# A hybrid decoder trunk on one core: element-wise work of the token mixers moves from GpSimd to VectorE and ScalarE

## Chip, core and metric

The kernel runs on one core of a Trainium2 chip. The metric is the device time of one execution in microseconds (us). The engines are TensorE (PE; its weight loads are PEld), VectorE (DVE), ScalarE (ACT), GpSimd (POOL) and SyncE (SP), which here issues the DMAs.

## What is computed

One inference step of a two-layer decoder for a prompt of 512 positions and 8 single-position samples, 520 columns in all. Each layer has a SwiGLU feed-forward block (FFN), a mixer with three branches, and a second FFN. The parts of the mixer that the change touches:

```python
def hgrn2_mixer(xq, xf, xi, xg, s0, lb, norm_g):
    k = (1.0 - lbh) * jax.nn.sigmoid(-zf)
    o, S = gla_chunked(heads(xq), k, heads(xi), logf, s0)   # S = f * S + k v^T
    o = o * lax.rsqrt(jnp.mean(o * o, axis=-1, keepdims=True) + EPS)
    o = o * norm_g.reshape(HG_HEADS, HG_DV)
    o = o.reshape(B, L, HG_WIDTH) * jax.nn.silu(xg)

def gmlp_mixer(xu, xv, ws, bs, ng, nb):
    u = jax.nn.gelu(xu)
    v = layer_norm(jax.nn.gelu(xv), ng, nb)
    return u * (tril(ws) v + bs), v          # in chunks of 128 positions

def s5_mixer(...):                           # complex diagonal recurrence
    _, h = lax.associative_scan(_ssm_combine, (a, bu), axis=1)
    y = real(c h) + d_skip * u
    z = jax.nn.gelu(y)
    zz = z @ glu_w + glu_b
    return zz[..., :S5_WIDTH] * jax.nn.sigmoid(zz[..., S5_WIDTH:])

def decoder_layer(...):
    gates = jax.nn.sigmoid(gate_cols).reshape(B, L, N_BRANCH, D_MODEL)
    merged = jnp.einsum('blnd,blnd->bld', gates, bproj)
    x = x + rms_norm(merged @ w_out, norm_g[3])
```

## The kernel before

Activations lie with channels on the 128 partitions and the 520 columns along the free axis, worked in two halves of 256 and 264 columns. Every large product is made of three matmuls: each weight block is loaded as `raw` (SP), cast to a high part `whi` (ACT, L98) and a low part `wlo` (raw minus whi, L102 on DVE or, with `share=True`, L232 on POOL through the helper `ptt`); each activation is split in the same way by `split` (high part on ACT, L110; low part on POOL, or on the engine that is passed, L111). `mm3` (L117, L118, L120) multiplies high with high, low with high and high with low.

Work that is not such a product runs as generators (`s5_scan`, `hgrn_head`) that are advanced from `tick` between weight blocks. The order on each engine is then set by a scheduler, which places instructions by a model of the engines, so an edit can move instructions that it does not name. Each engine executes its own queue strictly in that order.

A mixer goes through these steps:

- `s5_project` makes the S5 inputs. `s5_scan` (L776 on) works 8 steps per layer. In each, PE projects (L790), ACT copies the result to `w` (L792), DVE and POOL rotate it (L811 to L820), DVE scans it (L824), DVE and POOL rotate it back into `w` (L833 to L837), and PE multiplies `w` with tables (L846 to L848). A gelu follows (`gelu2`: square on ACT, L241; two operations on DVE, L244 and L245; tanh on ACT, L246; one on DVE, L247).
- `hgrn_head` runs once per head, 4 per layer. It has 7 levels; in each, PE makes a product of `q` and `k` (L1088), POOL multiplies `k` by the tree of decays (`ptt`, so the profile names L232), DVE multiplies `q` (L1091) and writes the masked result (L1092). The transpose of `k` (L1106) and the final products follow. Its inner function `state` updates two samples' states at a time: three POOL products on 128x256 tiles (`st` by `fs`, `vb` by `ks`, and their sum). `st` and `vb` arrive by DMA.
- `ev_f` and `ev_g` in `hgrn_operands` make `f`, `k` and `sg` for a head: sigmoids on ACT, scale and offset on DVE (L1003, L1004), `sg` on POOL. `stat` and `rstd` (L220 to L228) make the reciprocal root from column means on PE (L256).
- `s5_glu`, `gate`, `gmlp_values`, `gmlp_norm` and `gmlp_mix` follow, then the output product.

The two lines of the state update and of the gelu that matter most:

```python
self.ptt(st, st, bc(fs), ALU.mult)            # POOL, as are the next two
nc.vector.tensor_scalar(t, t, GELU_A, 1.0, ALU.mult, ALU.add)
nc.vector.tensor_tensor(t, t, x, ALU.mult)
```

Of the kernel before, what the change touches and what calls it, by code (L numbers as in the profile page):

```python
# [18 lines left out]
P = 128  # L19
# [23 lines left out]
class Trunk:  # L43
# [190 lines left out]
    def gelu2(self, out, x, pool, tag, bufs=1, scale=None, src=None):  # L234

        nc = self.nc
        shape = [P] + [int(n) for n in x.shape[1:]]
        n = x.shape[0]
        t = pool.tile(shape, F32, tag=tag, name=tag, bufs=bufs)[:n]
        if src is None:  # L240
            nc.scalar.activation(t, x, AF.Square)  # L241
        else:
            nc.scalar.activation(t, src, AF.Square, scale=scale)
        nc.vector.tensor_scalar(t, t, GELU_A, 1.0, ALU.mult, ALU.add)  # L244
        nc.vector.tensor_tensor(t, t, x, ALU.mult)  # L245
        nc.scalar.activation(t, t, AF.Tanh, scale=GELU_B)  # L246
        nc.vector.scalar_tensor_tensor(out, t, 1.0, x, ALU.add, ALU.mult)  # L247

    def stat(self, acc, half, mean, col=None):


        n = 2 + half
        v = self.pxt()
        mm = self.nc.tensor.matmul
        for i in range(n):
            mm(v[:, i:i + 1], acc[:, 128 * (i % 2):128 * (i % 2) + 128], mean, start=True, stop=True)  # L256
        if half:
# [458 lines left out]
    def mixer_units(self, l):  # L716
        return [lambda i=i, m=m: self.unit(self.t["w_in"][l, m], 8, 128, share=i % 2 == 0) for i, m in enumerate((0, 1, 2, 3, 8))]
# [50 lines left out]
    def s5_scan(self, l, pool):  # L768
# [32 lines left out]
        for s in range(n):  # L801
# [9 lines left out]
            self.ptt(tc_[:, 1], wp[:, 1], si[:, 1], ALU.mult)  # L811
            v.tensor_tensor(ta, wp, co, ALU.mult)
            v.tensor_tensor(tc_[:, 0], wp[:, 0], si[:, 0], ALU.mult)
# [19 lines left out]
            self.ptt(tc_[:, 1], ta[:, 1], si[:, 1], ALU.mult)  # L833
            v.tensor_tensor(tc_[:, 0], ta[:, 0], si[:, 0], ALU.mult)
# [46 lines left out]
    def s5_glu(self, l):  # L881
        nc, t = self.nc, self.t
        self.c = []
        for m in range(4):
# [9 lines left out]
            for half in (0, 1):  # L894
                s, b = self.tmph("sil", half), self.tmph("vb", half)
                p1, p2 = ps[half]
                nc.scalar.activation(s, p2, AF.Sigmoid, bias=self.glub[:, l * 8 + 4 + m:l * 8 + 5 + m])
                nc.vector.scalar_tensor_tensor(b, p1, self.glub[:, l * 8 + m:l * 8 + m + 1], s, ALU.add, ALU.mult)
                self.split(c[:, :, SL[half]], b)
# [73 lines left out]
    def hgrn_values(self, l, hh, pool, V):  # L973
# [12 lines left out]
        self.tok_proj("w_i", l, hh, evac, hh == 0)  # L986
# [4 lines left out]
    def hgrn_operands(self, l, h, pool):  # L991
# [5 lines left out]
        def ev_f(half, p):  # L997
# [5 lines left out]
            v.tensor_scalar(fs, fs, lb1, lb, ALU.mult, ALU.add)  # L1003
            v.tensor_scalar(ks, ks, lb1, None, ALU.mult)  # L1004
# [4 lines left out]
        def ev_g(half, p):  # L1009
# [3 lines left out]
            self.ptt(sg[:, SL[half]], a, b, ALU.mult)  # L1013
# [3 lines left out]
    def hgrn_head(self, l, h, V, q, k, f, sg, pool, last):  # L1017
# [60 lines left out]
        for lev in range(7):  # L1078
# [11 lines left out]
            self.ptt(kv, kv, Tr, ALU.mult)  # L1090
# [47 lines left out]
        for half in (0, 1):  # L1138
            st = self.stat(sqs[half], half, self.mean_h)
# [4 lines left out]
            self.split(ap[:, :, SL[half]], b)  # L1144
# [3 lines left out]
    def gmlp_values(self, l, pool):  # L1148
# [3 lines left out]
        for cg in range(2):  # L1152
            def evac(i, p):
# [4 lines left out]
                self.gelu2(self.vt[i][:n, 256 * cg:256 * cg + 256], x, pool, "gt", 2, rc, p)  # L1158
# [29 lines left out]
    def gmlp_mix(self, l, pool, fill):  # L1188
# [11 lines left out]
        for gr in range(4):  # L1200
# [24 lines left out]
            self.split(b[:, :, :NT], mx)  # L1225
# [3 lines left out]
    def mixer(self, l, xd, finish, ahead):  # L1229
# [8 lines left out]
        def head(h, done=0):  # L1238
# [7 lines left out]
            for block, ev in list(zip((8, 4, 12), evs))[done:]:  # L1246
                self.proj_block(l, block + h, ev, h == 0)
# [202 lines left out]
```

## Time and profile before

| | |
|---|---|
| median of 3 runs | 2754.24 us (2752.72 to 2756.12) |
| the profiled execution's own time | 2757.39 us |
| its span, first to last instruction | 2755.3 us |
| PE busy | 2673.8 us, 97% of the span |
| DVE / ACT / POOL busy | 1557.5 / 1014.9 / 795.2 us |

Busy is the time in which an engine had an instruction in work. Matmuls overlap in the pipeline, so the count of matmuls per microsecond says more of PE's pace than its busy time. In the trace each fp32 matmul of the small products appears twice. The profile's span and the runs' times differ by a few microseconds; differences are taken within the same kind.

### The profile page before, as it was taken

Reading aid. Unit: us, or ns where it says so; the run is one execution under the profiler, and the core shown is the slowest. Engines: PE = TensorE matmul, PEld = TensorE weight load, DVE = VectorE, ACT = ScalarE, POOL = GpSimd, SP = SyncE. Lnnn points to the kernel's source line nnn. Section 1 sums busy time; section 2 is a strip of 40 time slices with the busy share of each in tenths; the row PEclk is TensorE's granted clock in tenths of the full one; section 3 lists DMA queues with packets and bytes.
Section 4 is the critical chain, followed back from the end, with each engine's and each line's share of the span. In section 5 each row is a group of like instructions: output and inputs, shape, how many; then the busy total and the mean of one; then the engine's idle time right before and its main releaser. Section 6 shows DMA issues by size and latency. Waiting matters only on the chain. (4 is left out here: it accounts for less than half of the span.)

```text
span 2755.3 us, 54254 instructions
## 1 busy us (share of the span) xinstructions
PE 2673.8 (97%) x21976; PEld 2649.0 (96%) x21976; DVE 1557.5 (57%) x3127; ACT 1014.9 (37%) x2014; POOL 795.2 (29%) x1033
## 2 busy tenths in 40 slices
PE   7999999899999999999999999998999999999998
PEld 7999999889999999999999999998999999999998
DVE  7677867865574564344473434668555654634444
ACT  4344444333243353322343323433323334433232
POOL 5478812453221112011121101145521311301010
PEclk9999999999999999999999999999999999999999
DMA  4344543542232323232322222445332223222321
GB/s 135 102 141 148 160 135 121 182 126 83 86 93 92 116 77 93 93 92 100 93 77 93 90 95 93 131 135 156 98 100 86 87 92 120 84 89 88 99 91 54
DMA packets 131706, 291.16 MB, mean 106 GB/s; under 512 B 19024, under 2 KB 59760, under 8 KB 131456
## 3 DMA queue, kind: packets, MB, share of 16 engines
q1 hardware_dynamic: 131456, 287.70, 33.1%
q8 instruction: 173, 2.83, 0.4%
q14 instruction: 77, 0.63, 0.1%
HBM read 256.97 MB, written 30.67 MB: 104 GB/s over the span
## 5 line engine op out<-in xcount | busy, mean ns | idle before, releaser
L117 PE MATMUL mm<-h,whi 128*128 128x256 f32 (+1 forms) x4224 | 1057.9, 287 | 18.2 <-ACT h L298 7.0
L118 PE MATMUL mm<-h,wlo 128*128 128x256 f32 (+1 forms) x4224 | 1047.1, 284 | 1.1 <-DVE wlo L102 1.1
L117 PEld LDWEIGHTS mm<-h,whi 128*128 128x128 f32 x4224 | 801.6, 190 | 20.2 <-ACT h L298 7.0
L118 PEld LDWEIGHTS mm<-h,wlo 128*128 128x128 f32 x4224 | 804.0, 190 | 1.7 <-DVE wlo L102 1.6
L98 ACT CAST whi<-raw 128x1024 fp32r<-128x1024 f32 (+1 forms) x424 | 437.3, 1032 | 510.9 <-PE mm L120 432.7
L102 DVE TENSOR_TENSOR wlo<-raw,whi 128x1024 fp32r<-128x1024 f32 (+1 forms) x385 | 474.0, 1231 | 233.1 <-ACT whi L98 230.3
L120 PE MATMUL mm<-h,whi 128*128 128x256 f32 (+1 forms) x4224 | 594.5, 283 | 0.0
L120 PEld LDWEIGHTS mm<-h,whi 128*128 128x128 f32 x4224 | 543.1, 189 | 0.0
L111 POOL TENSOR_TENSOR hid<-vb,hid 128x256 fp32r<-128x256 f32 (+1 forms) x132 | 132.7, 1006 | 870.0 <-ACT hid L110 857.0
L117 PE MATMUL mm<-hid,whi 128*128 128x256 f32 (+1 forms) x1408 | 349.0, 284 | 3.6 <-ACT hid L110 3.6
L118 PE MATMUL mm<-hid,wlo 128*128 128x256 f32 (+1 forms) x1408 | 347.5, 283 | 0.0
L124 DVE TENSOR_TENSOR va<-mm,r 128x256 f32<-128x256 f32 (+1 forms) x320 | 136.1, 426 | 310.3 <-PE mm L120 304.0
L117 PEld LDWEIGHTS mm<-hid,whi 128*128 128x128 f32 x1408 | 265.6, 189 | 3.8 <-ACT hid L110 3.8
L118 PEld LDWEIGHTS mm<-hid,wlo 128*128 128x128 f32 x1408 | 266.2, 189 | 0.0
L120 PE MATMUL mm<-hid,whi 128*128 128x256 f32 (+1 forms) x1408 | 201.2, 283 | 0.3 <-DVE hid L111 0.3
L124 DVE TENSOR_TENSOR vb<-mm,r 128x256 f32<-128x256 f32 (+1 forms) x176 | 74.9, 425 | 192.5 <-PE mm L120 192.5
L120 PEld LDWEIGHTS mm<-hid,whi 128*128 128x128 f32 x1408 | 182.7, 189 | 0.5 <-DVE hid L111 0.5
L110 ACT CAST hid<-vb 128x256 fp32r<-128x256 f32 (+1 forms) x176 | 72.1, 410 | 280.4 <-DVE vb L403 277.1
L232 POOL TENSOR_TENSOR wlo<-raw,whi 128x1024 fp32r<-128x1024 f32 x39 | 94.8, 2432 | 226.5 <-ACT whi L98 226.5
L401 ACT ACTIVATE sil<-va 128x256 f32<-128x256 f32 (+1 forms) x176 | 73.7, 419 | 152.8 <-DVE va L124 149.1
L434 DVE TENSOR_TENSOR y<-mm,y 128x264 f32<-128x264 f32 (+1 forms) x128 | 54.2, 425 | 117.1 <-PE mm L120 116.6
L403 DVE TENSOR_TENSOR vb<-vb,sil 128x256 f32<-128x256 f32 (+1 forms) x176 | 83.6, 475 | 17.2 <-ACT sil L401 2.5
(462 smaller groups left out, 3792.2 us busy)
## 6 DMA issues: line engine op xcount, KB each, us to landing
raw<-in_w_up SPq DMA_DIRECT2D x176, 512.0 KB, 3.7
raw<-in_w_in SPq DMA_DIRECT2D x88, 512.0 KB, 3.6
raw<-in_w_down SPq DMA_DIRECT2D x64, 448.0 KB, 3.4
raw<-in_w_down SPq DMA_DIRECT2D x32, 512.0 KB, 3.5
tab<-tb SPq DMA_DIRECT2D x48, 256.0 KB, 2.3
tab<-tab SPq DMA_DIRECT2D x48, 256.0 KB, 3.4
raw<-in_w_branch SPq DMA_DIRECT2D x24, 512.0 KB, 3.7
raw<-in_w_out SPq DMA_DIRECT2D x16, 512.0 KB, 4.6
```

The costliest lines, as they stand in the source:

```text
L98: nc.scalar.copy(hi[:, :n], raw[:, :n])
L102: nc.vector.tensor_tensor(lo[:, :n], raw[:, :n], hi[:, :n].bitcast(F32), ALU.subtract)
L110: nc.scalar.copy(pair[:, 0], src)
L111: (lo_eng or nc.gpsimd).tensor_tensor(pair[:, 1], src, pair[:, 0].bitcast(F32), ALU.subtract)
L117: mm(out, wh, x[:, 0], start=first and k == 0, stop=False)
L118: mm(out, wl, x[:, 0], start=False, stop=False)
L120: mm(out, wh, x[:, 1], start=False, stop=last and k == n - 1)
L124: self.nc.vector.tensor_tensor(dst, p, self.rms(half), ALU.mult)
L232: self.nc.gpsimd.tensor_tensor(out, a, b, op)
L401: nc.scalar.activation(s, a, AF.Silu)
L403: nc.vector.tensor_tensor(b, b, s, ALU.mult)
L434: nc.vector.tensor_tensor(ys, pd, ys, ALU.add)
```

## The change

Work that GpSimd did in the mixers goes to other engines, and some operations are merged or placed elsewhere:

- `gelu2` squares with the scale sqrt(0.044715) on ACT and then needs one DVE operation in place of two; the square in `gmlp_values` reads the SBUF copy instead of PSUM.
- `state`: per sample, one ACT product (`st` by a column of `fs`) and one DVE operation (`vb` by a column of `ks`, plus `st`), on 128x128 tiles.
- The product of `k` in the levels, `sg`, the second half of both S5 rotations (now one 128x512 operation instead of a 128x256 on each engine), and the low parts in `s5_glu`, `hgrn_head` and `gmlp_mix` go to DVE.
- `wlo` of 7 weight blocks per layer goes from POOL to DVE (`share` no longer passed in the mixers).
- Scale and offset of `f` and `k` go from DVE to ACT.
- The 1e-6 of the head norm is added to the column means (2 or 3 columns) instead of to the squares (256 or 264 columns).

POOL keeps the gates' sum (`x<-x,vb`), the decay tree, small copies, `gmlp_norm`'s share, the low parts in the FFNs and in the output merge, and the FFNs' `wlo`.

```diff
     def gelu2(...)
-        if src is None:
-            nc.scalar.activation(t, x, AF.Square)
-        else:
-            nc.scalar.activation(t, src, AF.Square, scale=scale)
-        nc.vector.tensor_scalar(t, t, GELU_A, 1.0, ALU.mult, ALU.add)
-        nc.vector.tensor_tensor(t, t, x, ALU.mult)
+        nc.scalar.activation(t, x, AF.Square, scale=math.sqrt(GELU_A))
+        nc.vector.scalar_tensor_tensor(t, t, 1.0, x, ALU.add, ALU.mult)
         nc.scalar.activation(t, t, AF.Tanh, scale=GELU_B)
...
     def stat(...)
-        self.rstd(col, v[:, :n])
+        m = v[:, :n]
+        if eps is not None:
+            m = self.tmpt("rs_v", 2, 4)[:, :n]
+            self.nc.vector.tensor_scalar(m, v[:, :n], eps, None, ALU.add)
+        self.rstd(col, m)
...
     def mixer_units(self, l):
-        ... self.unit(self.t["w_in"][l, m], 8, 128, share=i % 2 == 0) ...
+        ... self.unit(self.t["w_in"][l, m], 8, 128) ...
...
-            self.ptt(tc_[:, 1], wp[:, 1], si[:, 1], ALU.mult)
             v.tensor_tensor(ta, wp, co, ALU.mult)
-            v.tensor_tensor(tc_[:, 0], wp[:, 0], si[:, 0], ALU.mult)
+            v.tensor_tensor(tc_, wp, si, ALU.mult)
...
-            self.ptt(tc_[:, 1], ta[:, 1], si[:, 1], ALU.mult)
-            v.tensor_tensor(tc_[:, 0], ta[:, 0], si[:, 0], ALU.mult)
+            v.tensor_tensor(tc_, ta, si, ALU.mult)
...
-                self.split(c[:, :, SL[half]], b)
+                self.split(c[:, :, SL[half]], b, nc.vector)
...
-        self.tok_proj("w_i", l, hh, evac, hh == 0)
+        self.tok_proj("w_i", l, hh, evac)
...
-            v.tensor_scalar(fs, fs, lb1, lb, ALU.mult, ALU.add)
-            v.tensor_scalar(ks, ks, lb1, None, ALU.mult)
+            nc.scalar.activation(fs, fs, AF.Identity, scale=lb1, bias=lb)
+            nc.scalar.activation(ks, ks, AF.Copy, scale=lb1)
...
-            self.ptt(sg[:, SL[half]], a, b, ALU.mult)
+            v.tensor_tensor(sg[:, SL[half]], a, b, ALU.mult)
...
         def state(b0):
-            bc = lambda a: a[:, b0:b0 + 2][:, :, None].to_broadcast([P, 2, P])
-            self.ptt(st, st, bc(fs), ALU.mult)
-            self.ptt(vb, vb, bc(ks), ALU.mult)
-            self.ptt(st, st, vb, ALU.add)
+            for b in range(2):
+                nc.scalar.activation(st[:, b], st[:, b], AF.Copy, scale=fs[:, b0 + b:b0 + b + 1])
+                v.scalar_tensor_tensor(st[:, b], vb[:, b], ks[:, b0 + b:b0 + b + 1], st[:, b], ALU.mult, ALU.add)
...
-            self.ptt(kv, kv, Tr, ALU.mult)
+            v.tensor_tensor(kv, kv, Tr, ALU.mult)
...
-            v.tensor_scalar(sq, sq, 1e-6, None, ALU.add)
...
-            st = self.stat(sqs[half], half, self.mean_h)
+            st = self.stat(sqs[half], half, self.mean_h, eps=1e-6)
...
-            self.split(ap[:, :, SL[half]], b)
+            self.split(ap[:, :, SL[half]], b, v)
...
-            self.split(b[:, :, :NT], mx)
+            self.split(b[:, :, :NT], mx, v)
...
-                self.proj_block(l, block + h, ev, h == 0)
+                self.proj_block(l, block + h, ev)
```

In all DVE gets 3219 instructions in place of 3129, ACT 2112 in place of 2016, POOL 781 in place of 1035; PE and SP keep 21086 and 922, in another order. Three places, in the first layer's mixer.

VectorE, the rotation back in the third scan step, before (`tc` is the rotated product, `w` what PE multiplies next, `va` an evacuation of a PSUM bank):

```order
L834 TENSOR_TENSOR tc__6906<-ta,tab 128x256
L102 TENSOR_TENSOR wlo<-raw,whi 128x1024
L247 SCALAR_TENSOR_TENSOR y<-sil,aux 128x144
L835 TENSOR_TENSOR ta<-ta,tab 128x512
L124 TENSOR_TENSOR va<-mm,r 128x256
L836 TENSOR_TENSOR w<-ta,tc__6906 128x2x128
L837 TENSOR_TENSOR w<-ta,tc__6906 128x2x128
```

and now:

```order
L832 TENSOR_TENSOR tc__6898<-ta,tab 128x512
L1011 TENSOR_TENSOR sg<-va,vb 128x256
L833 TENSOR_TENSOR ta<-ta,tab 128x512
L124 TENSOR_TENSOR va<-mm,r 128x264
L834 TENSOR_TENSOR w<-ta,tc__6898 128x2x128
L835 TENSOR_TENSOR w<-ta,tc__6898 128x2x128
```

The low part of a weight block no longer stands inside this step; `sg` does, and the product is twice as wide.

VectorE at the start of the mixer, the reciprocal root of the second half's norm (`rcol`, whose last operation PE waits for), before:

```order
L225 SCALAR_TENSOR_TENSOR rcol<-rs_s,rcol 128x3
L226 TENSOR_TENSOR rs_s<-rcol 128x3
L227 SCALAR_TENSOR_TENSOR rs_s<-rs_s,aux 128x3
L228 SCALAR_TENSOR_TENSOR rcol<-rs_s,rcol 128x3
L739 TENSOR_TENSOR up<-mm,r 128x66x4
```

and now:

```order
L225 SCALAR_TENSOR_TENSOR rcol<-rs_s,rcol 128x3
L226 TENSOR_TENSOR rs_s<-rcol 128x3
L227 SCALAR_TENSOR_TENSOR rs_s<-rs_s,aux 128x3
L102 TENSOR_TENSOR wlo<-raw,whi 128x1024
L228 SCALAR_TENSOR_TENSOR rcol<-rs_s,rcol 128x3
L102 TENSOR_TENSOR wlo<-raw,whi 128x1024
L739 TENSOR_TENSOR up<-mm,r 128x66x4
```

Two low parts that POOL made beside this chain now stand in it.

ScalarE at the first state updates (`V` are evacuations of PSUM banks, `w` the copy of a scan step's projection), before:

```order
L983 ACTIVATE V<-mm,rcol 128x128 x2
L792 COPY w<-aux 128x2x144 x2
L983 ACTIVATE V<-mm,rcol 128x128 x6
L983 ACTIVATE vs<-mm,rcol 8x128 x2
L792 COPY w<-aux 128x2x144 x2
```

and now:

```order
L1059 ACTIVATE st<-st,fs 128x128 x2
L981 ACTIVATE V<-mm,rcol 128x128 x2
L1059 ACTIVATE st<-st,fs 128x128
L792 COPY w<-aux 128x2x144
L1059 ACTIVATE st<-st,fs 128x128
L792 COPY w<-aux 128x2x144
L981 ACTIVATE V<-mm,rcol 128x128 x6
```

State products, which read tiles that come by DMA, now stand ahead of and between the copies of `w`.

## Rows read from the trace of the kernel before

**Rows 1.** The page: engines' busy time (share, instructions), and one group of its costliest.

```profile
PE 2673.8 (97%) x21976; PEld 2649.0 (96%) x21976; DVE 1557.5 (57%) x3127; ACT 1014.9 (37%) x2014; POOL 795.2 (29%) x1033
...
L102 DVE TENSOR_TENSOR wlo<-raw,whi 128x1024 fp32r<-128x1024 f32 (+1 forms) x385 | 474.0, 1231 | 233.1 <-ACT whi L98 230.3
```

**Rows 2.** Windows: stretch, length, each engine's busy us (count), PEclk, DMA share, GB/s.

```profile
480.00:640.00 160.00, 147.04 (x1148) 141.39 (x1148) 116.15 (x273) 57.12 (x137) 83.81 (x145) 0.96 0.47 143
500.00:520.00 20.00, 17.73 (x131) 17.14 (x129) 20.00 (x43) 5.88 (x17) 13.35 (x23) 0.91 0.67 204
...
640.00:960.00 320.00, 316.72 (x2642) 313.14 (x2642) 179.98 (x364) 106.25 (x196) 74.88 (x93) 1.00 0.31 94
1825.00:1985.00 160.00, 146.05 (x1143) 140.60 (x1143) 115.73 (x272) 56.97 (x137) 84.53 (x144) 0.96 0.46 142
```

**Rows 3.** Waits of PE, 480 to 640 us: total us, times, longest.

```profile
PE aux L847 <- issue: 3.2, 2, 2.0
PE aux L1106 <- POOL k L232: 1.8, 2, 1.3
PE aux L1088 <- POOL k L232: 1.6, 1, 1.6
...
PE aux L848 <- DVE w L837: 0.7, 3, 0.3
```

**Rows 4.** Timeline of VectorE, 462 to 508 us: start, duration, instruction.

```profile
462.18 1.62 DVE L221 TENSOR_SCALAR rcol<-rcol 128x3 f32<-128x3 f32 x1
463.83 0.16 DVE L222 TENSOR_TENSOR rs_s<-rcol 128x3 f32<-128x3 f32 x1
...
507.91 1.75 DVE L102 TENSOR_TENSOR wlo<-raw,whi 128x1024 fp32r<-128x1024 f32 x1
```

**Rows 5.** Timeline of GpSimd, 461 to 515 us.

```profile
461.39 2.38 POOL L232 TENSOR_TENSOR wlo<-raw,whi 128x1024 fp32r<-128x1024 f32 x1 [4.27 <-ACT whi L98]
...
514.44 1.02 POOL L232 TENSOR_TENSOR sg<-va,vb 128x264 f32<-128x264 f32 x1
```

**Rows 6.** One line's instructions, L813 and L124: durations min/median/max in ns, starts in us.

```profile
L813 DVE TENSOR_TENSOR tc__7030<-w,tab x1: 965/965/965, 514.8 to 514.8; 128x256 f32<-128x256 f32 x1
...
L813 DVE TENSOR_TENSOR tc__7678<-w,tab x1: 410/410/410, 550.7 to 550.7; 128x256 f32<-128x256 f32 x1
...
L124 DVE TENSOR_TENSOR va<-mm,r x320: 401/425/435, 34.3 to 2691.1; 128x256 f32<-128x256 f32 x156, 128x264 f32<-128x264 f32 x4
```

**Rows 7.** Groups on GpSimd, 480 to 640 us: busy us, mean ns, idle before.

```profile
L232 POOL TENSOR_TENSOR k<-k,TT 128x256 f32<-128x256 f32 x12 | 10.7, 893 | 6.2 <-PE aux L1088 6.1
L232 POOL TENSOR_TENSOR vb<-vb,ks 128x256 f32<-128x256 f32 x12 | 8.3, 688 | 7.1 <-DMA vb<-vd 7.1
L232 POOL TENSOR_TENSOR st<-st,vb 128x256 f32<-128x256 f32 x10 | 7.8, 782 | 0.5
...
L232 POOL TENSOR_TENSOR st<-st,fs 128x256 f32<-128x256 f32 x8 | 5.2, 649 | 5.8 <-DMA st<-in_state_hgrn 5.8
```

**Rows 8.** Groups on VectorE, 480 to 640 us.

```profile
L102 DVE TENSOR_TENSOR wlo<-raw,whi 128x1024 fp32r<-128x1024 f32 x15 | 20.5, 1370 | 0.7 <-ACT whi L98 0.7
...
L835 DVE TENSOR_TENSOR ta<-ta,tab 128x512 f32<-128x512 f32 x8 | 6.0, 749 | 0.6 <-POOL tc__6640 L232 0.6
...
L244 DVE TENSOR_SCALAR sil<-sil 128x144 f32<-128x144 f32 x16 | 5.6, 347 | 0.0
L1091 DVE TENSOR_TENSOR q<-q,TT 128x256 f32<-128x256 f32 x12 | 5.3, 443 | 4.9 <-PE aux L1088 4.9
...
L1118 DVE SCALAR_TENSOR_TENSOR S<-S,T,aux 128x128 f32<-128x128 f32 x6 | 2.0, 342 | 1.4 <-ACT S L1116 1.4
...
L1003 DVE TENSOR_SCALAR f<-f,lb,lb 128x256 f32<-128x256 f32 (+1 forms) x4 | 1.6, 405 | 0.0
...
L819 DVE TENSOR_TENSOR ta<-ta,tc__7320 128x256 f32<-128x256 f32 x1 | 1.1, 1090 | 0.0
...
L820 DVE TENSOR_TENSOR ta<-ta,tc__6906 128x256 f32<-128x256 f32 x1 | 0.6, 615 | 0.0
```

More of the change, by code (lines that the diff above doesn't have):

```diff
@@ L232, in ptt, with gelu2 @@
         self.nc.gpsimd.tensor_tensor(out, a, b, op)
-    def gelu2(self, out, x, pool, tag, bufs=1, scale=None, src=None):
+    def gelu2(self, out, x, pool, tag, bufs=1):
         nc = self.nc
@@ L239, in gelu2, with stat @@
         t = pool.tile(shape, F32, tag=tag, name=tag, bufs=bufs)[:n]
-        if src is None:
-            nc.scalar.activation(t, x, AF.Square)
-        else:
-            nc.scalar.activation(t, src, AF.Square, scale=scale)
-        nc.vector.tensor_scalar(t, t, GELU_A, 1.0, ALU.mult, ALU.add)
-        nc.vector.tensor_tensor(t, t, x, ALU.mult)
+        nc.scalar.activation(t, x, AF.Square, scale=math.sqrt(GELU_A))
+        nc.vector.scalar_tensor_tensor(t, t, 1.0, x, ALU.add, ALU.mult)
         nc.scalar.activation(t, t, AF.Tanh, scale=GELU_B)
         nc.vector.scalar_tensor_tensor(out, t, 1.0, x, ALU.add, ALU.mult)
-    def stat(self, acc, half, mean, col=None):
+    def stat(self, acc, half, mean, col=None, eps=None):
         n = 2 + half
@@ L716, in mixer_units @@
     def mixer_units(self, l):
-        return [lambda i=i, m=m: self.unit(self.t["w_in"][l, m], 8, 128, share=i % 2 == 0) for i, m in enumerate((0, 1, 2, 3, 8))]
+        return [lambda i=i, m=m: self.unit(self.t["w_in"][l, m], 8, 128) for i, m in enumerate((0, 1, 2, 3, 8))]
     def ffn_units(self, l, f):
@@ L1157, in evac @@
                 nc.scalar.activation(x, p, AF.Copy, scale=rc)
-                self.gelu2(self.vt[i][:n, 256 * cg:256 * cg + 256], x, pool, "gt", 2, rc, p)
+                self.gelu2(self.vt[i][:n, 256 * cg:256 * cg + 256], x, pool, "gt", 2)
             self.tok_proj("w_v", l, cg, evac)
```

## The prediction, made before the change was run

> **What bounds the kernel now.** I read the page first: PE is busy 97% of the span, every other engine far less [rows 1]. The change alters no matmul, so it can only give back time in which PE stands still or runs slowly. The windows tell where that is. From 640 to 960 us PE starts 2642 matmuls in 320 us, 8.256 a microsecond, and nothing is lost there. From 480 to 640 us, the first layer's S5 scan with the first two heads beside it, it starts 1148 in 160 us. At 8.256 a microsecond these need 139.0 us, so about 21.0 us are lost. In the second layer's copy of the stage 1143 need 138.4, and 21.6 are lost [rows 2]. Together 42.6 us: this is nearly all that the change can win.
>
> Of it 160 - 147.04 = 13.0 us and 160 - 146.05 = 14.0 us are idle time of PE in the records. The granted clock is 0.96 in both stages [rows 2], the mean of stretches at 2.4 and at 1.2 GHz; in 640 to 960 us, where PE does not stop, it is 1.00. That is 4% of 160, or 6.4 us a stage. The remaining 2.8 us I can't place.
>
> PE's waits tell what it stands for [rows 3]. The longest item is L847, the products of a scan step with `w`: the row says "issue", but the rotation on VectorE that writes `w` is the only long work ahead of it. Then come `k` from GpSimd (L1088, L1106: 1.8 + 1.6 = 3.4 us). VectorE is busy 20.00 of 20 us between 500 and 520 us [rows 2], so the scan is bound there by VectorE.
>
> **Why VectorE is slow there.** The same 128x256 product L813 takes 410 ns at 550.7 us, when GpSimd is between two operations, and 965 ns at 514.8 us, in the middle of GpSimd's `sg`, which runs from 514.44 for 1.02 us [rows 5, 6]. A 3-column operation, L221, takes 1.62 us instead of the next one's 0.16 while GpSimd works on `wlo` from 461.39 for 2.38 us [rows 4, 5]. L124 has the same number of elements, but one input in PSUM, and stays within 401 to 435 ns over 320 instructions [rows 6]. So in these rows VectorE is held up by GpSimd when both read SBUF operands, and moving work off GpSimd costs VectorE less than its own duration. The Trainium skill (SBUF — State Buffer, Who interferes with whom) says that a VectorE instruction with two SBUF inputs and a GpSimd instruction that reads SBUF exclude each other for a whole instruction. By that rule every moved microsecond would be time that VectorE could not use anyway, and the stage would win nearly all of its 42.6 us; the trace bears out the slowdown, but shows pairs that overlap, so I do not sum by it.
>
> **What moves, per stage (480 to 640 us).**
>
> - *GpSimd loses* the four groups of rows 7, 10.7 + 8.3 + 7.8 + 5.2 = 32.0 us, and 32 more instructions (16 scan products, 6 `sg`, 8 low parts, two first-level `k`) that I cost at the `k` row's 0.893: 28.6. That is 60.6 of 83.8 us.
> - *VectorE gains* 14 products of `k` and 14 of `sg` and low parts at L1091's 0.443: 12.4 us; 16 scan products that grow from 256 to 512 columns, 0.749 (L835) less 0.410 (L813): 5.4; 20 state operations of 128x128, which no row shows. From above L1118 bounds them, same shape but one input in PSUM, 0.342; from below half of L1091, 0.22. I take 0.30, nearer L1118 for the equal shape: 6.0. Sum 23.8 [rows 6, 8].
> - *VectorE loses* 16 L244 at 0.347, 5.6 us, and 8 of L1003 and L1004 at 0.405, 3.2: 8.8. The 1e-6 on fewer columns I leave uncounted. Net +15.0.
> - *Relief on VectorE.* The 15 `wlo` average 1.370 against 1.231 over all 385 [rows 1, 8]: 2.1 us. Of the 48 narrow scan operations 13 lie between 0.615 (L820) and 1.090 (L819) and sum to 10.9 us; at 0.41 they need 5.3, so 5.6. I take these 7.7; the share of GpSimd that stays lowers it, kinds that I did not count raise it. Ends: 0 and 15. VectorE then goes to 116.2 + 15.0 - 7.7 = 123.5 of 160 us: fuller, but not full.
> - *ScalarE gains* 8 operations for `f`, `k` and 20 state products. Bounds: 0.405 each as L1003, at most 0.65 as GpSimd's twice as wide product. At most 16.2 us on top of 57.12, so it stays under half of the stage and hides.
> - *Weight low parts.* Four of the seven per layer are due before 480 us. They add 4 x 1.23 us to VectorE, and the order puts one ahead of `rcol`'s last operation, for which PE waits. L221's 1.62 falls back to 0.16 there. +1.23 against -1.46: I count zero; ends -1.5 and +1.2 per layer.
>
> **What reaches PE, per stage.**
>
> - *Scan products.* The four groups of L847 and L848, from 3.2 us for the first to 0.7 for the last, sum to 5.6 us of waits for the rotation. The one of 2.0 us had a 1.75 us `wlo` inside the rotation [rows 3, 4], which the new order puts outside; GpSimd's slowdown and the hand-overs to it go. I credit two thirds, 3.7; ends 0 and 5.6.
> - *Products of `k`.* They take 0.443 instead of 0.893 and don't queue behind states on GpSimd, but on VectorE they stand ahead of the product of `q`. Two thirds of 3.4 us [rows 3]: 2.3; ends 0 and 3.4.
> - *The other waits*, the rest of the 13.0 us, are for VectorE's queue and for tables: nothing, as VectorE gets no emptier and no transfer gets shorter.
> - *A new wait.* GpSimd sat 7.1 us for `vb` and 5.8 us for `st` to land [rows 7]. Now ScalarE waits for `st`, with the copies of `w` and the weight casts behind it, and VectorE for `vb`, with the scan behind it; PE waits for both. Those queues have other work first, so most landings come in time. I charge 1.0; ends 0 and 12.9.
>
> That is 5.0 us of 13.0 per stage, 10.0 for both. With 37% of the stops gone I take 37% of the clock's loss, 0.37 x 12.8 = 4.7, and of the unplaced 2.8, 1.0. Outside the stages I credit 1.3 for shorter gelus and low parts. Sum -17.0. From the profiled execution's 2757.4 us this gives 2740.4; it stood 3.2 us above the median of the runs, so 2737 is the number for the median.
>
> **Rivals.**
>
> 1. *The waits only change their name.* The scheduler keeps PE's consumers close behind VectorE, and VectorE's load rises by 7.3 us a stage. Then L847 waits as long as before, and `k` is late because VectorE is. For it: VectorE at 20.00 of 20 [rows 2]. Against it: the slowed rows. The time is that of before, 2754 +- 5.
> 2. *VectorE becomes the bound, and the kernel slower.* If the relief is nothing, 15.0 us more stand in a queue that is already full from 500 to 520 us. If all of it lands on PE, and only the waits for GpSimd's `k` (3.4) go, each stage costs 11.6 more: 2754 + 23 = 2777. It decides where VectorE's busy time in the stage passes 131 us, as then it got the whole addition. Against it: VectorE has 43.9 us free there, and the slowdown of L813 is in the rows. The Trainium skill (Perfetto Trace Analysis, Optimizing Scalar/DVE Operations) advises to move work off a saturated VectorE, to ScalarE or even GpSimd, which is the other way round from this change; by that advice this rival holds. The rows agree that VectorE is saturated, for 20 us of the 160.
> 3. *Full relief.* VectorE's stalls vanish, PE does not stop and keeps 2.4 GHz: -42.6, 2712.
> 4. *The change does not take effect*, because the scheduler's new order undoes it. The order shows the instructions moved and 254 fewer on GpSimd, so I give this only a part of rival 1's chance.
>
> **How the numbers follow.** About 0.2%, 5.5 us, is what a measurement of this kernel tells from no change. The forecast, -6 to -32 us, gets 0.59; full relief, beyond -32, 0.14; the same waits under new names, within 5.5 us, 0.14; slower by VectorE 0.13. So faster 0.73, same 0.14, slower 0.13. The forecast's own range is 2722 to 2748. The range of 8 in 10 takes in full relief at 2712 and the unchanged case up to 2757, and leaves out the slower rival and the thin tail below.
>
> **What would show it.** Right: in the two stages matmuls rise above 1148 and 1143 in 160 us; waits for POOL `k` are gone; L813's 512-column successor takes near 0.7 us every time; `wlo` there averages below 1.30; the clock rises above 0.96. Wrong: L847 still waits 3 us or more, or PE or VectorE waits on DMA `vb` or ScalarE on `st` for over 2 us at a time; VectorE is busy over 131 us in a stage; or the stages gain and time goes elsewhere, as at the start of a mixer, where `rcol` would be more than 1.2 us later.

## The result, and the profile after

The changed kernel takes 2719.78 us (median of 4 runs, 2718.72 to 2720.74) where the kernel before took 2755.18 us beside it (2752.72 to 2757.23). The ratio is 0.987 with an interval of 0.9859 to 0.9882: 35.4 us faster, about twice the forecast gain of 17, inside the range of 2712 to 2757. The profiled spans are 2755.3 and 2719.0 us, 36.3 apart.

The page's busy line, which answers to [rows 1]:

```profile
PE 2664.9 (98%) x21976; PEld 2644.7 (97%) x21976; DVE 1564.0 (58%) x3217; ACT 1045.6 (38%) x2110; POOL 580.7 (21%) x779
```

GpSimd lost 214.5 us of busy time, and VectorE, which took most of that work, rose by 6.5 us. The windows of after, for the same matmuls as the mixer start of the first layer and as the two scan stages of [rows 2]:

```profile
core 0: us, PE busy (x) PEld busy (x) DVE busy (x) ACT busy (x) POOL busy (x), PEclk, DMA share, GB/s
432.40:476.20 43.80, 43.80 (x367) 43.46 (x366) 33.07 (x83) 21.24 (x43) 2.48 (x12) 1.00 0.43 132
476.20:621.70 145.50, 141.80 (x1147) 137.62 (x1146) 113.44 (x295) 62.84 (x160) 32.96 (x71) 0.98 0.52 156
1804.80:1949.50 144.70, 140.33 (x1143) 135.62 (x1142) 113.26 (x297) 63.03 (x160) 31.25 (x69) 0.99 0.51 157
```

Before, the first scan stage took 160 us for 1148 matmuls and the second 160 for 1143. They gained 14.4 us (with 0.1 taken off for the one matmul) and 15.3, 29.7 together. PE's idle time there fell from 13.0 to 3.7 us and from 14.0 to 4.4. VectorE's busy time fell too, from 116.15 to 113.44, although it does more.

The second place is the start of each mixer. The window and PE's waits of before, for the same matmuls as the first row of after above:

```profile
433.40:479.80 46.40, 44.03 (x366) 43.46 (x365) 31.15 (x82) 18.99 (x37) 14.81 (x18) 1.00 0.40 126
```

```profile
PE aux L256 <- DVE acc L366: 1.2, 1, 1.2
PE aux L270 <- DVE rcol L228: 1.1, 1, 1.1
```

Both waits are gone after, and the stretch is 2.6 us shorter; the second layer's goes from 47.5 to 44.8. So 5.3 us come from the mixer starts, and 29.7 + 5.3 = 35.0 of the 36.3 us are placed.

PE's waits of after in the first scan stage, all that the view lists, in place of [rows 3]:

```profile
PE aux L1085 <- ACT w L792: 1.5, 1, 1.5
PE aux L1085 <- DVE q L1088: 1.2, 1, 1.2
PE aux L845 <- POOL s_new L814: 0.4, 1, 0.4
PE aux L252 <- ACT sq L1130: 0.4, 1, 0.4
```

No wait for `k` from GpSimd is left, and none of the scan's products (L845 to L847 now) for the rotation. VectorE's groups in that stage, which answer to [rows 8] (columns as there):

```profile
L102 DVE TENSOR_TENSOR wlo<-raw,whi 128x1024 fp32r<-128x1024 f32 x14 | 17.1, 1224 | 0.4 <-ACT whi L98 0.4
L823 DVE TENSOR_TENSOR_SCAN ta<-rho,ta 128x128 f32<-128x128 f32 x32 | 11.6, 408 | 0.0
L1060 DVE SCALAR_TENSOR_TENSOR st<-vb,ks,st 128x128 f32<-128x128 f32 x20 | 6.4, 347 | 2.8 <-ACT st L1059 2.8
L833 DVE TENSOR_TENSOR ta<-ta,tab 128x512 f32<-128x512 f32 x8 | 5.6, 703 | 0.0
L811 DVE TENSOR_TENSOR ta<-w,tab 128x512 f32<-128x512 f32 x8 | 5.5, 690 | 4.6 <-ACT w L792 4.5
L1087 DVE TENSOR_TENSOR k<-k,TT 128x256 f32<-128x256 f32 x12 | 5.0, 420 | 1.8 <-PE aux L1085 1.5 <-issue 0.3
```

`wlo` went from 1370 to 1224 ns and the 512-column product L835 (now L833) from 749 to 703. The scan (L823) stood before at

```profile
L824 DVE TENSOR_TENSOR_SCAN ta<-rho,ta 128x128 f32<-128x128 f32 x32 | 13.4, 454 | 0.0
```

The moved operations cost about what the prediction put down: `k` 420 ns for 443, the state operation 347 for 300, a little above the upper bound of 342 that it gave.

### The profile page after: what moved, and what is told of

The parts are those of the page before. It is cut to its first block, busy times and chain, and to the rows that moved or that the text cites. A ratio compares the mean times of both kernels' runs of the same rounds, so it can differ in the third digit from the quotient of the medians.

```text
span 2719.0 us, 54122 instructions
## 1 busy us (share of the span) xinstructions
PE 2664.9 (98%) x21976; PEld 2644.7 (97%) x21976; DVE 1564.0 (58%) x3217; ACT 1045.6 (38%) x2110; POOL 580.7 (21%) x779
## 4 chain that ended last, share of the span: by engine, by line
PE 83%; issue 6%; DVE 6%; POOL 3%; DMA 2%; ACT 1%; SPq 0%; DVEq 0%; POOLq 0%; ACTq 0%
PE mm L117 25%; PE mm L120 24%; PE mm L118 24%; PE mm L943 1%; PE mm L944 1%; PE mm L945 1%; PE aux L1085 1%; PE aux L270 1%; PE aux L252 1%; DVE h L302 1%; PE aux L682 0%; DMA raw<-in_w_in 0%; DVE acc L213 0%; PE aux L790 0%; DVE wlo L102 0%
## 5 line engine op out<-in xcount | busy, mean ns | idle before, releaser
L102 DVE TENSOR_TENSOR wlo<-raw,whi 128x1024 fp32r<-128x1024 f32 (+1 forms) x399 | 486.9, 1220 | 236.4 <-ACT whi L98 233.6
L124 DVE TENSOR_TENSOR va<-mm,r 128x256 f32<-128x256 f32 (+1 forms) x320 | 136.1, 426 | 302.6 <-PE mm L120 298.0
L124 DVE TENSOR_TENSOR vb<-mm,r 128x256 f32<-128x256 f32 (+1 forms) x176 | 74.9, 425 | 192.4 <-PE mm L120 192.4
L434 DVE TENSOR_TENSOR y<-mm,y 128x264 f32<-128x264 f32 (+1 forms) x128 | 54.2, 426 | 113.9 <-PE mm L120 113.4
L945 PE MATMUL mm<-whi,h 128*128 128x256 f32 (+1 forms) x320 | 90.5, 283 | 0.0
```

What stands on the lines that cost most here:

```text
L102: nc.vector.tensor_tensor(lo[:, :n], raw[:, :n], hi[:, :n].bitcast(F32), ALU.subtract)
L124: self.nc.vector.tensor_tensor(dst, p, self.rms(half), ALU.mult)
L434: nc.vector.tensor_tensor(ys, pd, ys, ALU.add)
L945: nc.tensor.matmul(p, self.h[k][:, 1, tk], wh, start=False, stop=k == KD - 1)
```

## The experiments

All kernels are built on after. The theories: **A**, GpSimd's reads of SBUF slow VectorE, and VectorE feeds PE late; **B**, PE waited for results that came late through GpSimd's own queue; **C**, VectorE has less to do (shorter gelu, scale and offset on ScalarE). The kernel before, timed beside each group, had medians of 2754.67 to 2757.53 us, so differences of up to 3 us between groups say nothing. "Stage" is a scan stage: the same 1143 to 1148 matmuls each time. Line numbers shift by a few from kernel to kernel.

**Useless work put back on GpSimd, first try.** Two kernels issued products or memsets from constants where GpSimd's work had been:

```diff
+    def idle(self, n):
+        i2 = self.ident[:, None].to_broadcast([P, 2, P])
+        for _ in range(n):
+            self.nc.gpsimd.tensor_tensor(self.scr, i2, i2, ALU.mult)
...
+            self.idle(1)
             v.tensor_tensor(ta, wp, co, ALU.mult)
```

> The changed kernel plus products on GpSimd that nobody reads: 128x256 from SBUF constants into a scratch tile, one for each operation that the change took away (3 per state pair, 1 per level, 2 per scan step, 1 per sg and low part). Theory A (GpSimd's reads of SBUF slow VectorE wherever the two meet): most of the 29 us that the two scan stages won comes back, 2735 to 2750, with VectorE's 512-column rotation products near 1 us again. Theory B (PE had waited for results that came late through GpSimd's queue): nobody waits for these, so 2717 to 2725. Theory C (VectorE simply has less to do, by the shorter gelu and the scaling that went to ScalarE): 2717 to 2725.

> As idle_tt, but each product is two fills of the scratch tile, which read nothing. Theory A: GpSimd busy without reading costs little, 2717 to 2726, and VectorE's durations stay as in the changed kernel. If it costs as much as idle_tt, it is not the reads but GpSimd being busy at all, or the order that moved. Theories B and C: 2717 to 2725.

Measured: 2814.2 us (2810.7 to 2814.45) with products, 2787.95 (2786.17 to 2789.44) with memsets. Both missed their purpose. Operations on constants depend on nothing, so the scheduler put them at the start of the program (the products run from 2.0 to 242.5 us), where PE then waited for GpSimd's first results. PE's waits of the kernel with products, 0 to 527 us:

```profile
PE mm L119 <- POOL wlo L239: 26.8, 3, 20.0
PE aux L689 <- POOL er L661: 26.0, 1, 26.0
```

In the kernel with products the first stage, with GpSimd at 31.96 us, took 142.7 us at a clock of 1.00, no more than in after. The times say nothing on A, B or C. The kernel with memsets still shows, at the start of the program, what GpSimd does to VectorE when it writes without reading: 13 `wlo` of 128x1024 that overlap memsets alone take 1209 to 1227 ns, as without them, while of the 96 of the whole program that overlap only GpSimd instructions with an input some take up to 1880. Ten other VectorE operations beside memsets, nine of them with one input, are 0.1 to 0.23 us longer than others of their kind.

**Useless work on GpSimd, tied to its place.** Each product now reads something made or loaded there; two per scan step, three per pair of sample states, one per level of a head:

```diff
+            self.ptt(self.scr, co[:, 1], si[:, 1], ALU.mult)
...
+            for _ in range(3):
+                self.ptt(self.scr, vb, vb, ALU.mult)
...
+            self.ptt(self.scr.rearrange(...)..., Tl, Tr, ALU.mult)
```

> After's kernel plus useless products on GpSimd that nobody reads, this time each with an operand that is made at its place in the mixer: 2 of 128x256 per scan step, 3 per pair of sample states, one per level of a head. VectorE, ScalarE and PE keep after's instructions, so nothing that PE waits for comes from GpSimd. A (GpSimd's two-input work slows VectorE): the 512-column products of the rotation (L811, L832), 0.68 to 0.72 us in after, average above 0.8 us, PE's idle time in the first scan stage goes from 3.7 us back above 7, and the time is 2732 to 2750 us. B (PE waited for results that came late through GpSimd's own queue) and C (VectorE has less to do): no result that PE needs is touched, 2717 to 2724 us.

Measured: 2748.74 us (2741.02 to 2751.58), ratio 0.9975 (0.9964 to 0.9985). PE, VectorE and ScalarE execute the same instructions in the same order as in after. Its two stages:

```profile
475.60:631.50 155.90, 146.12 (x1148) 139.72 (x1147) 131.01 (x294) 63.02 (x161) 81.82 (x140) 0.97 0.49 147
1813.90:1971.50 157.60, 146.25 (x1144) 140.44 (x1143) 130.70 (x294) 63.00 (x160) 81.04 (x138) 0.96 0.48 146
```

GpSimd went from 32.96 to 81.82 us, near the 83.81 of before, and VectorE's unchanged work from 113.44 to 131.01: 17.6 us for 48.9, or 0.36 for 1. The stages are 10.4 and 12.9 us longer, so 23.3 of the 29.7 us are gone again, with no useful result moved. (In span the profiled execution is at 2741.7 us against after's 2719.0; by the medians of the runs the difference is 29.0 us.) PE's idle time in the first stage is 9.8 us, above the 7 that A foretold. That fits A; C is excluded as the main cause, since VectorE kept its shorter work. Where the slowdown sits, the groups of tile `ta` in the first stage (columns: instructions, ns least/median/most, first and last start), after and then this kernel (the scan, the first product of the rotation, and its second sum in the same step):

```profile
L823 DVE TENSOR_TENSOR_SCAN ta<-rho,ta x32: 394/408/426, 478.5 to 571.3; 128x128 f32<-128x128 f32 x32
L811 DVE TENSOR_TENSOR ta<-w,tab x8: 681/688/707, 476.5 to 562.5; 128x512 f32<-128x512 f32 x8
L819 DVE TENSOR_TENSOR ta<-ta,tc__6898 x1: 416/416/416, 501.5 to 501.5; 128x256 f32<-128x256 f32 x1
```

```profile
L825 DVE TENSOR_TENSOR_SCAN ta<-rho,ta x32: 392/402/743, 478.0 to 582.0; 128x128 f32<-128x128 f32 x32
L813 DVE TENSOR_TENSOR ta<-w,tab x8: 673/680/1095, 476.0 to 570.1; 128x512 f32<-128x512 f32 x8
L821 DVE TENSOR_TENSOR ta<-ta,tc__6903 x1: 992/992/992, 500.9 to 500.9; 128x256 f32<-128x256 f32 x1
```

Medians hardly move; single instructions take up to twice as long or more. As the order is the same, each VectorE instruction of the first stage can be compared with itself in after. Of the 212 whose inputs all lie in SBUF 51 are more than 0.1 us longer, by 0.41 us in the median. Of the 83 that have an input in PSUM none is longer by more than 0.02 us, though 50 of them overlap a GpSimd instruction with an input. One kind of each sort in this kernel, of the same shape (`aux` lies in PSUM):

```profile
L1121 DVE SCALAR_TENSOR_TENSOR S<-S,T,aux x6: 334/341/348, 560.4 to 618.4; 128x128 f32<-128x128 f32 x6
L1065 DVE SCALAR_TENSOR_TENSOR st<-vb,ks,st x20: 328/346/770, 513.3 to 612.8; 128x128 f32<-128x128 f32 x20
```

In after the longest of these are 348 and 353 ns. All six of the first kind overlap GpSimd's work. So GpSimd being busy is not enough to slow VectorE here; where VectorE's inputs lie makes the difference. A's finer expectation, a mean above 0.8 us for the 512-column products, missed: L811 has 736 ns, and the eight of L832 average about 0.70 us, as the slowdown falls on many kinds a little. A part of B came with it: PE waited 1.7 us for a small copy to `w` in GpSimd's fuller queue.

**One-input copies in place of the useless products**, same places, same order on PE, VectorE and ScalarE (shown for the states; the products in the scan steps and levels likewise):

```diff
-                self.ptt(self.scr, vb, vb, ALU.mult)
+                g.tensor_copy(self.scr, vb)
```

> The run with useless products on GpSimd (2748.7 us), with a one-input copy of 128x256 in the place of each two-input product, at the same places; PE, VectorE and ScalarE have the same instructions in the same order. If any GpSimd instruction that reads SBUF holds up VectorE, for as long as it runs, VectorE's busy time in the first scan stage rises above after's 113.4 by about 0.36 us for each us that GpSimd's rises, and the time is 2732 to 2748 us, the lower the shorter a copy is than a product. If it takes a two-input product on GpSimd, VectorE stays within 2 us of after and the time is 2717 to 2724 us.

Measured: 2725.89 us (2723.96 to 2729.38). Between the two expectations:

```profile
478.10:625.90 147.80, 141.83 (x1148) 136.45 (x1147) 118.97 (x295) 63.06 (x160) 65.98 (x140) 0.99 0.52 155
```

VectorE rises by 5.5 us for 33.0 us of GpSimd, 0.17 for 1. One-input work on GpSimd holds VectorE up too, half as much for each microsecond: 30 of the 212 are longer, by 0.20 us in the median, and again none of the 83.

**One part undone at a time**, each on after. PE's idle time and the granted clock of the two stages, first and second, stand beside the medians, as a stage's length mixes both:

| undone | median, us | PE idle, us | clock |
|---|---|---|---|
| nothing (after) | 2719.78 | 3.7 and 4.4 | 0.98 and 0.99 |
| weight low parts | 2717.49 | 3.4 and 2.6 | 1.00 and 1.00 |
| gelu | 2723.63 | 5.0 and 5.6 | 0.98 and 0.99 |
| rotation | 2723.08 | 6.6 and 6.7 | 1.00 and 1.00 |
| product of `k` | 2732.22 | 8.1 and 8.4 | 0.97 and 0.97 |
| sample states | 2725.52 | 6.2 and 5.4 | 0.99 and 0.98 |
| low parts and `sg` | 2721.14 | 3.0 and 4.3 | 1.00 and 0.98 |

Of these only the ratio of `k` (0.9902 to 0.9932) lies clear of after's interval (0.9859 to 0.9882); the others overlap it.

Weight low parts back on GpSimd (seven per layer):

```diff
-        ... self.unit(self.t["w_in"][l, m], 8, 128) ...
+        ... self.unit(self.t["w_in"][l, m], 8, 128, share=i % 2 == 0) ...
-        self.tok_proj("w_i", l, hh, evac)
+        self.tok_proj("w_i", l, hh, evac, hh == 0)
```

> The changed kernel with the seven low parts of weights per layer back on GpSimd. Theory A: the 2.6 us that each start of a mixer won (which the prediction counted at zero) are lost again, as the 3-column operation behind GpSimd's low part takes 1.6 us again: 2724 to 2728. Theory B: no result of GpSimd is late there, 2718 to 2722. Theory C: VectorE loses 8.6 us of work per layer, so no slower, 2715 to 2720.

Measured: 2717.49 us (2716.04 to 2721.02), not told apart from after. The total lies below A's and B's ranges and in C's; but VectorE is busier in the stage, not less (114.82 us for 113.44), so it does not speak for C. The mixer start is as slow as before, with the same two waits, and the stage behind it is shorter:

```profile
432.40:478.80 46.40, 44.06 (x367) 43.49 (x366) 30.28 (x78) 22.05 (x46) 14.25 (x19) 1.00 0.41 127
478.80:620.60 141.80, 138.44 (x1148) 134.58 (x1147) 114.82 (x296) 64.63 (x160) 30.91 (x69) 1.00 0.53 161
```

```profile
PE aux L252 <- DVE acc L366: 1.2, 1, 1.2
PE aux L270 <- DVE rcol L228: 1.1, 1, 1.1
```

So the placement of these low parts is what took the waits away at the mixer start. In the stage PE idles 3.4 us, as in after (3.7), but the clock is 1.00 instead of 0.98: 145.5 x 0.02 = 2.9 of the 3.7 us.

The gelu of before:

```diff
-        nc.scalar.activation(t, x, AF.Square, scale=math.sqrt(GELU_A))
-        nc.vector.scalar_tensor_tensor(t, t, 1.0, x, ALU.add, ALU.mult)
+        nc.scalar.activation(t, x, AF.Square)
+        nc.vector.tensor_scalar(t, t, GELU_A, 1.0, ALU.mult, ALU.add)
+        nc.vector.tensor_tensor(t, t, x, ALU.mult)
```

> After's kernel with the gelu of before in `gelu2` (square without scale, then two VectorE operations): 20 to 30 more VectorE operations of 0.3 to 0.45 us in each mixer, nothing back on GpSimd. A: the relief on VectorE covers it nearly all, 2718 to 2725 us. B: nothing, 2717 to 2722 us. C (the gain is VectorE's shorter work): most of the gain in the scan stages is lost again, 2733 us or more.

Measured: 2723.63 us (2719.67 to 2725.87); the stages 147.0 and 145.7 us. C gave the shorter gelu most of the gain: that fell. By the medians it is worth about 4 us, as A said, but the intervals overlap.

The rotation's second half back on GpSimd:

```diff
-            v.tensor_tensor(tc_, wp, si, ALU.mult)
+            self.ptt(tc_[:, 1], wp[:, 1], si[:, 1], ALU.mult)
+            v.tensor_tensor(tc_[:, 0], wp[:, 0], si[:, 0], ALU.mult)
```

> After's kernel with the second half of both S5 rotations on GpSimd again: 16 products of 128x256 per layer, and VectorE's products shrink from 512 to 256 columns. A: VectorE's rotation is slowed again while GpSimd works on the other half, and PE waits for `w` at its products: 6 to 12 us lost over both layers, 2725 to 2732 us. C (VectorE's load sets the time): VectorE has 5 us less to do per stage, 2714 to 2719 us. B: the wait for the half from GpSimd comes back, 2720 to 2726 us.

Measured: 2723.08 us (2722.26 to 2726.39). VectorE is at 113.42 us in the first stage, as in after (113.44): the smaller products and the slowdown cancel. The time is in B's range and 2 us below A's: VectorE waits 2.7 us in all, in five places, for GpSimd's half, and PE 0.9 us at a scan product (L847). PE's longest wait is for the product of `q` (2.5 us). The stages are 146.0 and 145.1 us, only 0.5 and 0.4 above after's, but that is the clock's doing: PE's idle time rose by 2.9 and 2.3 us, and the clock is 1.00 in both instead of 0.98 and 0.99, which gives back about as much (2.9 and 1.4 us by the same rule as above).

The product of `k` back on GpSimd:

```diff
-            v.tensor_tensor(kv, kv, Tr, ALU.mult)
+            self.ptt(kv, kv, Tr, ALU.mult)
```

> After's kernel with the product of `k` in the 7 levels of each head on GpSimd again, 28 products per layer. GpSimd's queue is short now, without the states. A (slower VectorE): 14 of the 61 us of GpSimd's work in a scan stage are back, 2723 to 2729 us. B (late results of GpSimd): the waits of PE for `k` at L1088 and L1106 come back, 3 us in each layer, 2724 to 2728 us with GpSimd `k` in PE's waits. C: VectorE has 6 us less per stage, 2714 to 2719 us.

Measured: 2732.22 us (2730.65 to 2732.75), above what any theory said; the stages 152.4 and 151.4 us. PE's waits in the first:

```profile
PE aux L1085 <- POOL qs L1033: 3.7, 1, 3.7
PE aux L1085 <- ACT w L792: 1.4, 1, 1.4
PE aux L1085 <- POOL k L232: 1.3, 3, 0.7
PE aux L1103 <- POOL k L232: 0.9, 2, 0.5
```

B's waits are back with 1.3 + 0.9 = 2.2 us a stage. The largest names a copy of GpSimd, but the timeline of that moment (ScalarE, VectorE, PE; columns start, us, engine) tells it differently:

```profile
589.94 0.69 ACT L1059 ACTIVATE st<-st,fs 128x128 f32<-128x128 f32 x2 [2.44 <-DMA st<-in_state_hgrn]
590.38 0.64 DVE L1060 SCALAR_TENSOR_TENSOR st<-vb,ks,st 128x128 f32<-128x128 f32 x2 [1.50 <-ACT st L1059]
590.94 0.43 DVE L124 TENSOR_TENSOR q<-mm,r 128x264 f32<-128x264 f32 x1
591.28 0.42 DVE L1088 TENSOR_TENSOR q<-q,TT 128x256 f32<-128x256 f32 x1
591.84 1.94 PE L1085 MATMUL aux<-q,k 128*128 128x64 f32 x8 [3.73 <-POOL qs L1033]
```

ScalarE waits for a state to land, VectorE waits for ScalarE, and the product of `q` that PE reads stands behind it in VectorE's queue until 591.70. The copy `qs` is no input of this product, and `k` was ready at 587.80. I read the 3.7 us as that chain; no run took the chain away to prove it.

The sample states back on GpSimd:

```diff
-            for b in range(2):
-                nc.scalar.activation(st[:, b], ...)
-                v.scalar_tensor_tensor(st[:, b], vb[:, b], ...)
+            self.ptt(st, st, bc(fs), ALU.mult)
+            self.ptt(vb, vb, bc(ks), ALU.mult)
+            self.ptt(st, st, vb, ALU.add)
```

> After's kernel with the sample states on GpSimd again: three products of 128x256 per pair of samples, 30 in the first scan stage, 21 us of GpSimd's work; ScalarE loses 20 operations there and VectorE 20 of 0.347 us (6.9 us). A (GpSimd's reads slow VectorE, by 17.6 us of VectorE for 48.9 us of GpSimd in the run with useless products, that is 0.36 for 1): VectorE gets 7.6 us of slowdown for the 6.9 us it loses, and so only the queue on GpSimd counts; 2718 to 2724 us. B (results late through GpSimd's queue): the state products stand ahead of the small copies that heads need, and PE waits for them in each layer, as for `qs` 3.7 us with the product of `k` on GpSimd; 2724 to 2732 us. C (VectorE's load): 2712 to 2718 us.

Measured: 2725.52 us (2724.09 to 2726.85), in B's range and 1.5 above A's. VectorE is at 115.14 us in the first stage though 20 operations left it, about as A's 0.36 foretold (7.6 on and 6.9 off make 0.7 more; it is 1.7 more). PE's waits in the stage:

```profile
PE aux L845 <- issue: 1.9, 2, 1.7
PE aux L1028 <- ACT w L792: 1.6, 1, 1.6
PE aux L1069 <- POOL st L232: 1.0, 1, 1.0
```

One wait of 1.0 us for GpSimd's state is B's, smaller than said. How much of the loss is A's and how much B's, the run does not tell.

Low parts and `sg` back on GpSimd (`self.split(..., b)` without the engine, `self.ptt` for `sg`):

> After's kernel with the low parts in `s5_glu`, `hgrn_head` and `gmlp_mix` and the product `sg` on GpSimd again: 14 operations in the first scan stage, each two-input and 0.42 to 0.49 us on VectorE. A: 12 us of GpSimd's work cost VectorE 4 us and free 6 us, so the stage stays within 1.5 us; 2717 to 2723 us. B: these products are all read by PE after GpSimd, 2723 to 2730 us with POOL `c` or POOL `sg` in PE's waits.

Measured: 2721.14 us (2720.08 to 2723.08), as A said; of B's waits one of 0.4 us for GpSimd's `sg` is there. The two stages:

```profile
476.90:619.50 142.60, 139.62 (x1147) 134.93 (x1146) 111.42 (x281) 63.19 (x161) 44.58 (x85) 1.00 0.54 161
1803.10:1949.90 146.80, 142.54 (x1144) 137.73 (x1144) 111.55 (x282) 63.35 (x160) 44.33 (x83) 0.98 0.53 156
```

**Further in the same direction.** The norm of the gmlp branch wholly on VectorE:

```diff
-            e = v if i % 2 else g
+            e = v
```

> The changed kernel with the gmlp norm's products and sums all on VectorE (GpSimd did every other row tile). Theory A: VectorE's 512-wide operations there take 0.68 instead of 1.78 us, so that stretch ends earlier although VectorE has more of them, and PE's wait for va of 1.9 us per layer with the half-clock stretch behind it goes: 2713 to 2717. Theory B: GpSimd's share was parallel work, taking it away makes VectorE later: 2720 to 2724.

Measured: 2714.78 us (2710.66 to 2715.66), ratio to before 0.9848 (0.9831 to 0.9865). This is in A's range. After has one wait of 1.9 us at this place in each layer, which this kernel doesn't have:

```profile
PE mm L117 <- DVE va L124: 1.9, 1, 1.9
```

The stretch of the first layer in after, and then in this kernel:

```profile
773.40:814.50 41.10, 39.23 (x312) 38.87 (x311) 30.52 (x48) 12.66 (x23) 14.61 (x12) 0.96 0.28 91
771.00:812.00 41.00, 40.85 (x339) 40.49 (x338) 29.65 (x56) 12.66 (x23) 5.67 (x7) 1.00 0.32 100
```

PE starts 27 more matmuls in the same time. Its order is that of after in the whole program, so each matmul can be compared with itself: over this stretch PE gains 3.2 us in each layer, which covers the 5.0 us of the medians.

Both edits, this one and the weight low parts back on GpSimd:

> After's kernel with both edits that won by themselves: the norm of the gmlp branch on VectorE alone (2714.8), and the seven low parts of weights per layer on GpSimd as before (2717.5). If the two gains add, as they lie in different stretches (2117 and 480 us of the first layer's kind), 2710 to 2714 us; if either needs the gap of the other, 2714 to 2718 us.

Measured: 2714.85 us (2712.47 to 2715.84), no sign that they add, though the 2.3 us in question are within what two groups differ by. With the norm alone the clock in the stages is already 0.99 and 1.00, so the low parts win less there, and still lose their 2.6 us at the mixer start. The one-line edit is as good as both, 5.0 us below after by medians; the two intervals of the ratio overlap a little (0.9865 against 0.9859).

## Why the prediction was right in direction and short by half

- **What bounds the kernel: right.** 42.6 us were lost in the two stages. By the same pace, 1147 / 8.256 = 138.9 us of 145.5 and 1143 / 8.256 = 138.4 of 144.7, 6.6 + 6.3 = 12.9 us are still lost; 29.7 came back, where the sum had about 16.
- **Relief on VectorE: the mis-sized term**, taken as 7.7 between ends of 0 and 15. By the sum's own additions, 116.15 + 15.0 - 113.44 = 17.7 us are missing. 1.4 of these are a `wlo` that the stage no longer holds (14 for 15), and 1.3 the 1e-6 operations that I left uncounted. About 15.0 remain, the upper end. I had counted the two kinds whose rows were visibly slow and left the others at nothing. The 32 scans fell from 454 to 408 ns (1.5 us), and the run with useless work shows slowed instructions in nearly every kind that reads SBUF alone, and in none with an input in PSUM. A mean hides them: in that run four scans of 32 are slowed and move it only from 408 to 433 ns. The measured rate gives the same size: GpSimd lost 50.9 us in the stage (I had put 60.6), and 0.36 x 50.9 is 18.3.
- **Credits on PE: too small for that reason.** I gave 5.0 us of idle time a stage; 9.3 and 9.6 came. Two thirds of the waits for the rotation and for `k` were credited, and all are gone. "The other waits" got nothing, "as VectorE gets no emptier", but the list holds only 3.5 us in all now, against 13.0 us of idle time. One reading was loose: of the 5.6 us that I put down to the rotation, 0.9 stand in the list under a copy of GpSimd, `qs`.
- **The new wait: right, and with its size.** I charged 1.0 us a stage. PE's wait for DVE `q` is 1.2 us in the first and 2.0 in the second, and in the trace it ends with the chain foretold: VectorE at L1060 had waited 2.08 and 2.81 us for ScalarE's `st`, which waited for the DMA. By the letter that is one of the prediction's signs of being wrong (VectorE waiting on ScalarE's `st` for over 2 us at a time). The sign was drawn too tight: PE lost 1.2 and 2.0 us by it, and the stages still won 14.4 and 15.3. Its signs of being right all came.
- **Clock.** I took back 4.7 us. From 0.96 it went to 0.98 and 0.99: 6.4 - 2.9 and 6.4 - 1.4, 8.5 us, which is 3.8 more.
- **Mixer start: counted zero, was 5.3 us,** beyond the end of 1.5 per layer that I had set. The price of `wlo` on VectorE (+1.23 each) and the slowed L221 (-1.46) were set against each other. But PE's waits of 1.2 and 1.1 us for `acc` and `rcol` went altogether, though VectorE's busy time there rose from 31.15 to 33.07 us. The run with the low parts back on GpSimd returns both waits.
- **Rivals.** Waits that only change their name: fell. VectorE as the bound: fell, its mark of 131 us was never near (113.4); the run with useless work reached 131.0 and was still 6 us under before. No effect: fell. Full relief, 2712, was nearest: 2719.8 is past the forecast's own range by 2 us, on that side. That rival's words, PE does not stop and keeps 2.4 GHz, are true for all but 3.7 and 4.4 us and two short stretches a stage or fewer.

What is shown of the causes: GpSimd's work alone, without use and with the other engines' order unchanged, takes back 23.3 of the 29.7 us of the stages, and only VectorE instructions that read SBUF alone get longer by it (A). B is seen in that run as a wait of 1.7 us a stage, and with `k` and the states back; with `k` back it is 2.2 us a stage. The parts undone singly move the median by -2.3 to +12.4 us, but each also moves the order and the clock, so I do not share out the 35 us among them.

Why the state of the chain lands late can be read in part, in after's first stage (the last products with the older state, SyncE's issues, and ScalarE):

```profile
581.98 0.56 PE L1068 MATMUL aux<-qs,st 128*128 128x1 f32 x4
583.30 0.34 SPq L876 DMA_DIRECT2D out_s_sample<-s_new  x1
584.20 0.41 SPq L1050 DMA_DIRECT2D st<-in_state_hgrn  x1
588.27 0.69 ACT L1059 ACTIVATE st<-st,fs 128x128 f32<-128x128 f32 x2 [4.72 <-DMA st<-in_state_hgrn]
```

There are two buffers for `st`, and by the kernel's order this load takes the one whose state PE reads until 582.54. SyncE issues the load 1.7 us later, behind the store of `s_new`, for which it had sat since 579.6 while GpSimd made `s_new`. ScalarE can start 4.1 us after the issue. What the stage would be without that chain no run shows.

The Trainium skill (SBUF — State Buffer, Who interferes with whom) says that a VectorE instruction with two SBUF inputs contends with a GpSimd instruction that reads SBUF. The runs agree in kind, for products and for copies, and the 83 instructions with an input in PSUM stayed as they were. Its whole-instruction lock would have won nearly all of the 42.6 us by the prediction's working; 29.7 came. The section of the Trainium skill that the prediction cites for its second rival (Perfetto Trace Analysis, Optimizing Scalar/DVE Operations) adds that moving work between VectorE and GpSimd might not help, as they share a read port. The prediction left that out; with it the advice speaks less plainly for that rival, and here the move off GpSimd did help.

## What to carry to other kernels

Where two engines slow each other, moving work from one to the other is not paid by its duration: here 50.9 us left GpSimd in a stage, most of it to VectorE, and VectorE became 2.7 us less busy. Look at the longest instruction of each kind beside the median, as means hide a few doubled ones, and tell instructions with an input in PSUM, which were not slowed here, from those that read SBUF alone. To measure such a coupling, add useless work whose operand ties it to its place, and see that the other engines' order stays the same.

## What the runs showed that I had not expected

- One-input copies on GpSimd cost VectorE 0.17 us for each microsecond, products 0.36.
- What a stop of PE costs depends on the clock in the microseconds after it. After's first stage has two stretches at the lower level, 1.2 GHz, of 3.4 us each; the first begins 1.7 us after PE's 1.5 us wait ended at 524.4, the second 1.1 us after its 1.2 us wait ended at 589.8:

```profile
526.10:529.50 3.40, 3.40 (x18) 3.40 (x16) 2.44 (x7) 0.61 (x2) 0.11 (x1) 0.50 0.53 134
590.90:594.30 3.40, 3.40 (x18) 3.40 (x18) 1.58 (x4) 0.36 (x2) 0.00 (x0) 0.51 0.23 60
```

Each loses half of its length. The kernel with the low parts undone has both outcomes in one run: PE idles 142.6 - 139.62 = 3.0 us in the first stage, with the clock at 1.00, and 146.8 - 142.54 = 4.3 in the second, at 0.98. The stages differ by 4.2 us, 2.9 of them from the clock. A change of a few us in such a kernel can be no more than that. The kernel with the gmlp norm on VectorE shows it too: up to the edited place, at 779 us, all four compute engines have after's instructions in after's order, and yet its first stage takes 144.2 us for after's 145.5, at a clock of 0.99 for 0.98.
